# New priorities for both layers of a two-layer attention trunk, a mask that closes its score group, and work moved between ScalarE and VectorE

## The chip, the core and the metric

The kernel runs on one core of a Trainium2 chip. The metric is the time of one execution on the device, in microseconds (us). The engines of the core work at the same time, each through its own queue, in order: TensorE (PE, matrix products; its weight loads are listed as PEld), VectorE (DVE), ScalarE (ACT), GpSimd (POOL), and SyncE (SP), whose queue issues all loads and stores here. "span" is the time from the first to the last instruction of the profiled execution.

## The reference

256 positions of width 1024 go through two layers and a last RMSNorm, all in float32. Both layers have this form:

```python
hn = rmsnorm(h, norm_g[i])
q, k, v, z = split_proj(hn, w_in)            # one projection; 16 heads of 64
q, k = apply_rope(q, cos, sin), apply_rope(k, cos, sin)
o = attention(q, k, v)
o = o.reshape(B, S, MIX_WIDTH) * jax.nn.silu(z)
h = h + o @ w_out[i]
```

The first layer attends within a window of 128 positions, with 2 key and value heads and a learned sink for each query head that enters the softmax's sum. The second has 4 key and value heads and blocks of 256 keys. With 256 positions there is only one block, so it is causal attention over all of them.

## The kernel before

**Data.** Activations stand transposed: 8 tiles of 128 features by 256 positions. Weights come in 54 pieces of 512 KB, each 128 x 1024 (8 tiles of 128 x 128), in the order in which they are used: per layer query weights for the first half of the heads (q0), keys and values (kv), the second half (q1), the gate z in two halves (z0, z1), and the output projection in two halves (o0, o1); in the second layer kv comes before q0. All are loaded on SP's queue in this order (L84 to L90) into five raw buffers (`wraw`, NRAW = 5). A load waits until its buffer is free.

**Precision.** A float32 product is made from three matmuls in a faster format (`triple`, L136). The weight piece is split (`split`, L96): ScalarE copies its high part (`whi`, L108), and VectorE subtracts it to get the low part (`wlo`, L109). The activations are split in the same way (`split_h`, L147). Then come high x high, high x low and low x high (L140 to L142). For the pieces listed in `NATIVE`, nothing is split; TensorE multiplies float32 directly (L138), with unsplit activations `xf` (L155), and the piece keeps its raw buffer until TensorE is done with it. There are NHI = 7 buffers for high parts and NLO = 7 for low parts. With PACE = 2, the high part of a piece also waits until the low part of the piece two before it is written (L111).

Pieces are numbered in the order of `split` calls in the program: 0 to 3 are q0 of the first layer, 4 and 5 kv, 6 to 9 q1, 10 to 13 z0, 14 to 17 z1, 18 to 25 the output projection; 26 to 29 are kv of the second layer, 30 to 33 q0, 34 to 37 q1, 38 to 41 z0, 42 to 45 z1, and the rest the output projection.

**Statistics.** The squares of the input are summed, TensorE adds them over the partitions (L175), VectorE and GpSimd make the reciprocal root (L177, L179), and TensorE spreads it over all partitions (L182). It is multiplied into the rotation tables `csr` (L280), with which queries and keys are rotated (`rope`, L216): a shuffle and a multiplication on VectorE, and a second multiplication and an addition on VectorE or, for the entries in `RPL`, on GpSimd (L227, L228).

**Attention.** It goes in units of 4 heads by 128 queries: for each half c of the heads, u picks 4 of its 8 heads and b the first or the second 128 queries, so 8 units a layer. A unit with b = 1 sees 256 keys, one with b = 0 sees 128. In `attn` (L314), TensorE first adds the mask to the one score buffer (`sc`, L328), by a product of an identity with the mask in bf16, two matmuls over all of the unit's keys; then it adds the scores (L332). VectorE takes the maximum (L334), and ScalarE the exponentials with their sums (L343). VectorE makes the reciprocal (L346) and scales the four heads' probabilities (L348). TensorE transposes them (L353), ScalarE copies the transpose out of PSUM (L355), and TensorE multiplies by the values (L357). VectorE multiplies by the gate (L363), and the result is split for the output projection (L365, L366). There is one PSUM buffer for scores, one for the output `o`, two for transposes and three for projections (`mm`).

**Order.** Every instruction carries a priority, set by `at(...)` around each step from the tables `PRI0` and `PRI1` (plus 100 in the second layer). A planner orders the instructions before the kernel runs: it simulates the engines with durations of its own, and on each engine takes, of the instructions that are then ready and have their buffers, the one with the lowest number. On the chip, each engine follows that order strictly. The names in the tables are: `sq0`, `skv`, `sz0`, `so0` and so on for the splits of weights, `q0`, `kv`, `z0`, `o0` for the matmuls, `a0` and `a1` for the attention of each half, `st` for the statistics, `r0`, `r1`, `rk` for the rotations, `e0`, `e1` for what follows the gate's matmuls, and `f0`, `f1` for what follows the output projection's. `ORDER` and `ORDER1` give the order of the four units (b, u) in each half.

Of the kernel before, what the change touches and what calls it, by code (L numbers as in the profile page):

```python
# [17 lines left out]
T = S // P  # L18
TCX = {'schedule_with_timeline_sim': True}
SYNC = mybir.DependencyInfo(mybir.DependencyClass.Sync, mybir.DependencyReason.DATA)  # L20
PACE = 2
NATIVE = (7, 9, 11, 13, 15, 17, 31, 33, 35, 37, 39, 41)
RPL = [(0, 1, 0), (0, 1, 1), (1, 'k'), (1, 1, 0), (1, 1, 1)]
GLP = [(0, 0), (1, 0), (1, 1)]
SZP = [(0, 0), (0, 3), (1, 1)]
NRAW, NHI, NLO = 5, 7, 7
PRI0 = {'tr': -185.1, 'skv': -345.0, 'st': -372.0, 'kv': -93.4, 'sq0': -378.2, 'q0': -54.6, 'sz0': -416.4, 'z0': -41.1, 'a0': -142.2, 'sq1': -73.6, 'q1': -125.3, 'a1': -156.4, 'sz1': -158.0, 'z1': -31.1, 'so0': -360.9, 'o0': 17.2, 'so1': -103.2, 'o1': -39.6, 'r0': -138.0, 'r1': 21.5, 'rk': -107.9, 'p0': -118.5, 'p1': 29.8, 'e0': -99.9, 'e1': -247.7, 'f0': -197.9, 'f1': -254.0}
PRI1 = {'r0': -102.1, 'r1': -128.1, 'tr': 25.5, 'skv': -2.9, 'st': -281.7, 'kv': -97.4, 'sq0': -95.7, 'q0': -83.6, 'sz0': -20.3, 'z0': -7.5, 'a0': -176.2, 'sq1': -58.7, 'q1': -73.4, 'a1': -177.4, 'sz1': -74.6, 'z1': 87.9, 'so0': 80.5, 'o0': -32.3, 'so1': -88.6, 'o1': 91.0, 'rk': -31.6, 'p0': -215.2, 'p1': -14.3, 'e0': -145.1, 'e1': -189.1, 'f0': -90.9, 'f1': -119.3}
NPT = 3
NMM, NTR, NSC = 3, 2, 1  # L30
NW = 9
ORDER = [(0, 0), (1, 0), (1, 1), (0, 1)]
ORDER1 = [(0, 0), (0, 1), (1, 0), (1, 1)]
STEP = 0.1
EPS = 1e-05
NEG = -1e+30
# [3 lines left out]
def trunk(ctx: ExitStack, tc: tile.TileContext, xT, gf, sinks, consts, masks, wkva, w, out):  # L40
# [104 lines left out]
        return act.tile([P, 2, 2, S], F32R, name="quad", bufs=6)  # L145

    def split_h(layer, k, hs):  # L147
        if k == 0:
            xf.append(act.tile([P, KT, S], F32, name="xf", bufs=1))
        if k % 2 == 0:  # L150
            q = quads()
            hs += [q[:, 0], q[:, 1]]
        hi, lo = hs[k][:, 0], hs[k][:, 1]
        gc = g[:, layer, k:k + 1]
        nc.scalar.activation(xf[layer][:, k], h[:, k], AF.Copy, scale=gc)  # L155
        nc.scalar.activation(hi, h[:, k], AF.Copy, scale=gc)
        nc.vector.scalar_tensor_tensor(lo, h[:, k], gc, hi.bitcast(F32), op0=OP.mult, op1=OP.subtract)

# [33 lines left out]
    for layer in range(2):  # L192
# [18 lines left out]

        def block(ps, hw, j, k, width):
            wh, wl = cols(hw, j, k, width)
            triple(ps, wh, wl, hs[k][:, 0], hs[k][:, 1], xf[layer][:, k], k == 0, k == KT - 1)

        def rope(aps, pool=False, out=None):  # L216
            n = sum(x.shape[1] for x in aps)
# [96 lines left out]
        def attn(c, b, u, qs):  # L314
            nk = (b + 1) * P
            h0 = 8 * c + 4 * u
            if b == 0:
                mask = mkb[:, 2:3]
            else:
                mask = mkb[:, 1:3] if layer == 0 else mkb[:, 3:5]  # L320
            mask = mask.rearrange("p k s -> p (k s)")
            nm = work.tile([P, 4], F32, name="nm", bufs=4)
            rs = work.tile([P, 4], F32, name="rs", bufs=4)
            ri = work.tile([P, 4], F32, name="ri", bufs=4)
            p = work.tile([P, 4, nk], F32, name="pb" if b else "pa", bufs=2)
            sc = psum.tile([P, 2, 512], F32, name="sc", bufs=NSC)[:, :, :2 * nk].rearrange("p r (i k) -> p r i k", i=2)
            for par in range(2):
                nc.tensor.matmul(sc[:, par], mkb[:, 0], mask[:, None].to_broadcast([P, 2, nk]), start=True, stop=False)  # L328
            for n in range(4):
                i, par = n // 2, n % 2  # L330
                half = slice(64 * par, 64 * par + 64)
                nc.tensor.matmul(sc[:, par, i], qs[half, 2 * u + i, b * P:(b + 1) * P], ks[half, (h0 + n) // per, :nk],  # L332
                                 start=False, stop=i == 1)
            nc.vector.tensor_reduce(nm.rearrange("p (i r) -> p r i", r=2), sc, axis=mybir.AxisListType.X, op=OP.max,  # L334
                                    negate=True)
            scs = [sc[:, n % 2, n // 2] for n in range(4)]
            if layer == 0:
                es = work.tile([P, 4], F32, name="es", bufs=4)
                nc.vector.tensor_tensor(nm, nm, nsink[:, h0:h0 + 4], op=OP.min)
                nc.vector.tensor_add(es, nm, sink[:, h0:h0 + 4])  # L340
                nc.scalar.activation(es, es, AF.Exp)
            for n in range(4):
                nc.scalar.activation(p[:, n], scs[n], AF.Exp, bias=nm[:, n:n + 1], accum_out=rs[:, n:n + 1])  # L343
            if layer == 0:
                nc.vector.tensor_add(rs, rs, es)
            nc.vector.reciprocal(ri, rs)  # L346
            for n in range(4):
                nc.vector.tensor_scalar(p[:, n], p[:, n], ri[:, n:n + 1], None, op0=OP.mult)  # L348
            po = psum.tile([P, 2, P], F32, name="o", bufs=1)
            for kt in range(b + 1):  # L350
                pt = psum.tile([P, 4, P], F32, name="tr", bufs=NTR)
                for n in range(4):
                    nc.tensor.transpose(pt[:, n], p[:, n, kt * P:(kt + 1) * P], ident)  # L353
                pT = work.tile([P, 4, P], F32, name="pT", bufs=NPT)
                nc.scalar.activation(pT, pt, AF.Copy)  # L355
                for par in range(2):
                    nc.tensor.matmul(po[64 * par:64 * par + 64], vs[:, kt, h0 // per], pT[:, par::2],  # L357
                                     start=kt == 0, stop=kt == b)
            if (c, u) not in gt:
                gt[c, u] = quads()  # L360
            sl = slice(b * P, (b + 1) * P)
            gf = work.tile([P, 2, P], F32, name="gf")
            nc.vector.tensor_mul(gf, po, sz[:, 4 * c + 2 * u:4 * c + 2 * u + 2, sl])  # L363
            gh, gl = gt[c, u][:, :, 0, sl], gt[c, u][:, :, 1, sl]
            last[0] = nc.scalar.activation(gh, gf, AF.Copy)  # L365
            (nc.gpsimd if (c, u) in GLP else nc.vector).tensor_sub(gl, gf, gh.bitcast(F32))  # L366

        def zproj(c):
            with at(B + PRI["sz%d" % c]):
                hw = split(jz[c])  # L370
            with at(B + PRI["z%d" % c]):
                for f in range(4):
                    ps = psum.tile([P, S], F32, name="mm", bufs=NMM)
                    for k in range(KT):
                        c0 = f % 2 * P
                        wh, wl = part(hw[f // 2 * 2 + k // 4], k % 4, c0)
                        triple(ps, wh, wl, hs[k][:, 0], hs[k][:, 1], xf[layer][:, k], k == 0, k == KT - 1)
                    with at(B + PRI["e%d" % c]):
                        z = work.tile([P, S], F32, name="z")
                        th = work.tile([P, S], F32, name="th")  # L380
                        nc.vector.tensor_mul(z, ps, rh)
                        nc.scalar.activation(th, z, AF.Tanh)  # L382
                        if (c, f) in SZP:
                            nc.gpsimd.tensor_mul(th, th, z)  # L384
                            nc.gpsimd.tensor_add(sz[:, 4 * c + f], th, z)
                        else:
# [76 lines left out]
                                              o[:, 4 * i:4 * i + 4].rearrange("p k s -> p (k s)"))  # L463

        def attn_c(c, qs):
            for i, (b, u) in enumerate(ORDER if c == 0 else ORDER1):
                with at(B + PRI["a%d" % c] + STEP * i):
                    attn(c, b, u, qs)

# [83 lines left out]
```

## Time and profile before

| | |
|---|---|
| median of 3 runs | 244.24 us (241.94 to 244.81) |
| profiled execution, its own time | 243.5 us |
| its span | 241.7 us |
| mean granted TensorE clock | 0.984 |
| HBM read | 30.39 MB |

The rows of the profile read as follows. A group of instructions has its line, engine and operation, output<-input tiles, shapes and count, then the busy time, the mean of one in ns, and the idle time of the engine just before them with what ended it. A row of the timeline has the start, the duration, the engine, the line, and in brackets the idle time before it and its releaser. A row of the chain of waits has start, duration and instruction. A row of a windows table has, for each engine, busy time and instruction count, then the granted clock, the busy share of the DMA engines and GB/s. A row on waits has the total time, the number of times and the longest, in us.

### The profile page before, as it was taken

The numbers are of one execution on the slowest core, as the hardware profiler recorded it, in microseconds if no ns is written. First come the engines' busy times: TensorE is split into PE (matmuls) and PEld (weight loads), VectorE is DVE, ScalarE is ACT, GpSimd is POOL, SyncE is SP. The second block draws the span as 40 slices with busy tenths as digits, with TensorE's granted clock in tenths as the row PEclk, the third lists the DMA queues.
The fourth block names the chain that finished last, engine by engine and source line by source line (L and its number), as shares of the span: only waits on it lengthen the run. The fifth ranks groups of instructions, "written<-read, shape, count | busy, mean of one in ns | idle before, by whom it ended". The sixth has DMA issues, their size and how long they took to land.

```text
span 241.7 us, 4064 instructions
## 1 busy us (share of the span) xinstructions
PE 226.8 (94%) x1511; PEld 188.8 (78%) x1511; DVE 157.8 (65%) x321; ACT 125.2 (52%) x310; POOL 62.3 (26%) x64
## 2 busy tenths in 40 slices
PE   8979999999999999769999999999599999999990
PEld 4879989877678878559999988968487869687780
DVE  3899956938767867528972757585756556465363
ACT  7984245265765634529960624462656535474231
POOL 1872033232053011100741500030813103003241
PEclk9999999999999999999999999999799999999996
DMA  6998664444754222004743345247551420000022
GB/s 181 326 387 269 223 170 148 168 153 139 251 161 125 74 102 88 0 1 134 241 150 89 91 153 168 69 157 240 169 175 41 136 87 0 3 0 0 3 86 87
DMA packets 10244, 31.71 MB, mean 131 GB/s; under 512 B 1264, under 2 KB 2160, under 8 KB 10224
## 3 DMA queue, kind: packets, MB, share of 16 engines
q1 hardware_dynamic: 10224, 31.45, 40.5%
q8 instruction: 12, 0.20, 0.3%
q14 instruction: 8, 0.07, 0.1%
HBM read 30.39 MB, written 1.05 MB: 130 GB/s over the span
## 4 chain that ended last, share of the span: by engine, by line
PE 62%; DMA 15%; ACT 9%; DVE 8%; issue 2%; SPq 2%; POOL 1%; POOLq 0%; ACTq 0%; DVEq 0%
DMA wraw<-w 15%; PE mm L138 8%; PE mm L142 6%; PE mm L141 6%; PE mm L140 6%; PE tr L353 5%; PE sc L332 5%; PE o L357 5%; DVE wlo L109 4%; ACT whi L108 4%; PE mm L400 3%; PE mm L401 3%; PE mm L399 3%; PE mm L436 2%; PE mm L438 2%
## 5 line engine op out<-in xcount | busy, mean ns | idle before, releaser
L108 ACT ACTIVATE whi<-wraw 128x1024 fp32r<-128x1024 f32 (+2 forms) x45 | 44.7, 999 | 49.8 <-DMA wraw<-w 33.4
L109 DVE TENSOR_TENSOR wlo<-wraw,whi 128x1024 fp32r<-128x1024 f32 (+2 forms) x45 | 53.7, 1197 | 23.4 <-ACT whi L108 23.2
L140 PE MATMUL mm<-quad,whi 128*128 128x256 f32 x176 | 55.0, 315 | 0.8 <-ACT whi L108 0.8
L141 PE MATMUL mm<-quad,whi 128*128 128x256 f32 x176 | 50.1, 289 | 0.0
L142 PE MATMUL mm<-quad,wlo 128*128 128x256 f32 x176 | 49.2, 286 | 0.8 <-DVE wlo L109 0.8
L138 PE MATMUL mm<-xf,wraw 128*128 128x256 f32 x192 | 48.8, 388 | 0.0
L138 PEld LDWEIGHTS mm<-xf,wraw 128*128 128x128 f32 x192 | 34.3, 192 | 5.1 <-issue 1.4
L140 PEld LDWEIGHTS mm<-quad,whi 128*128 128x128 f32 x176 | 33.8, 193 | 3.3 <-ACT whi L108 1.3
L141 PEld LDWEIGHTS mm<-quad,whi 128*128 128x128 f32 x176 | 33.5, 192 | 2.5 <-issue 1.9
L142 PEld LDWEIGHTS mm<-quad,wlo 128*128 128x128 f32 x176 | 33.0, 190 | 1.9 <-DVE wlo L109 1.5
L366 POOL TENSOR_TENSOR quad<-gf,quad 128x256 fp32r<-128x256 f32 x12 | 10.5, 873 | 61.6 <-ACT quad L365 61.6
L355 ACT ACTIVATE pT<-tr 128x512 f32<-128x512 f32 x24 | 13.7, 594 | 21.7 <-PE tr L353 20.0
L334 DVE TENSOR_REDUCE nm<-sc 128x4 f32<-128x512 f32 (+1 forms) x16 | 15.2, 953 | 10.0 <-PE sc L332 10.0
L227 POOL TENSOR_TENSOR t<-t,csr 128x512 f32<-128x512 f32 x5 | 6.4, 1280 | 50.6 <-DVE t L223 46.9
L399 PE MATMUL mm<-quad,whi 128*128 128x256 f32 x64 | 17.7, 290 | 1.0 <-ACT quad L365 1.0
L332 PE MATMUL sc<-ks,qs 64*128 64x256 f32 (+1 forms) x128 | 18.6, 355 | 0.0
L400 PE MATMUL mm<-quad,whi 128*128 128x256 f32 x64 | 18.3, 290 | 0.2 <-POOL quad L366 0.2
L401 PE MATMUL mm<-quad,wlo 128*128 128x256 f32 x64 | 18.1, 287 | 0.0
L166 POOL TENSOR_TENSOR sq<-sq 128x256 f32<-128x256 f32 x14 | 14.7, 1052 | 8.4 <-ACT sq L164 7.8
L343 ACT ACTIVATE pb<-sc,nm 128x256 f32<-128x256 f32 x32 | 14.8, 472 | 3.7 <-DVE nm L334 3.7
L332 PEld LDWEIGHTS sc<-ks,qs 64*128 64x128 f32 x128 | 10.9, 186 | 6.7 <-issue 6.1
L384 POOL TENSOR_TENSOR th<-th,z 128x256 f32<-128x256 f32 x6 | 7.2, 1203 | 33.7 <-ACT th L382 33.7
(107 smaller groups left out, 412.1 us busy)
## 6 DMA issues: line engine op xcount, KB each, us to landing
wraw<-w SPq DMA_DIRECT2D x50, 512.0 KB, 4.5
wraw<-wkva SPq DMA_DIRECT2D x2, 512.0 KB, 8.6
out<-of SPq DMA_DIRECT2D x4, 256.0 KB, 2.2
wraw<-w SPq DMA_DIRECT2D x3, 256.0 KB, 3.8
hg<-xT SPq DMA_DIRECT2D x2, 256.0 KB, 5.7
wraw<-gf SPq DMA_DIRECT2D x1, 512.0 KB, 3.5
hg<-xT SPq DMA_DIRECT2D x3, 128.0 KB, 3.5
cst<-consts SPq DMA_DIRECT2D x1, 320.0 KB, 9.1
```

Of the source, the lines that this page charges most:

```text
L108: ia = nc.scalar.activation(a[:, c0:c1], r[:, c0:c1], AF.Copy)
L109: ib = nc.vector.tensor_sub(b[:, c0:c1], r[:, c0:c1], a[:, c0:c1].bitcast(F32))
L138: nc.tensor.matmul(ps, wh, x, start=start, stop=stop)
L140: nc.tensor.matmul(ps, wh, xh, start=start, stop=False)
L141: nc.tensor.matmul(ps, wh, xl, start=False, stop=False)
L142: nc.tensor.matmul(ps, wl, xh, start=False, stop=stop)
L332: nc.tensor.matmul(sc[:, par, i], qs[half, 2 * u + i, b * P:(b + 1) * P], ks[half, (h0 + n) // per, :nk], start=False, stop=i == 1)
L334: nc.vector.tensor_reduce(nm.rearrange("p (i r) -> p r i", r=2), sc, axis=mybir.AxisListType.X, op=OP.max, negate=True)
L343: nc.scalar.activation(p[:, n], scs[n], AF.Exp, bias=nm[:, n:n + 1], accum_out=rs[:, n:n + 1])
L399: nc.tensor.matmul(ps, wh, gh, start=k == 0, stop=False)
L400: nc.tensor.matmul(ps, wh, gl, start=False, stop=False)
L401: nc.tensor.matmul(ps, wl, gh, start=False, stop=k == 3)
```

## The change

- The priorities in `PRI0` and `PRI1` are all new, and the order of units is now given for each layer and half (`ORDERS`).
- PACE goes from 2 to 1, NHI from 7 to 9, and NLO from 7 to 5.
- `NATIVE` lists 10 pieces in place of 12, others in part.
- In `attn` the scores come first and the mask closes the group. In the second layer the mask covers only the last 128 keys, the diagonal block.
- For the units in `PSC`, ScalarE scales the probabilities in place of VectorE. For those in `PEV`, VectorE copies the transposes in place of ScalarE.
- `RPL`, `GLP` and `SZP`, which send work to GpSimd, have new entries, now by layer and unit: 3 rotations in place of 5, 10 subtractions in place of 12, and 6 gates as before.
- `xf` is written only in a layer that has a native piece among its projections; both layers have some.

```diff
-PACE = 2
-NATIVE = (7, 9, 11, 13, 15, 17, 31, 33, 35, 37, 39, 41)
-RPL = [(0, 1, 0), (0, 1, 1), (1, 'k'), (1, 1, 0), (1, 1, 1)]
-GLP = [(0, 0), (1, 0), (1, 1)]
-SZP = [(0, 0), (0, 3), (1, 1)]
-NRAW, NHI, NLO = 5, 7, 7
-PRI0 = {'tr': -185.1, 'skv': -345.0, 'st': -372.0, 'kv': -93.4, 'sq0': -378.2, 'q0': -54.6, 'sz0': -416.4, 'z0': -41.1, 'a0': -142.2, 'sq1': -73.6, 'q1': -125.3, 'a1': -156.4, 'sz1': -158.0, 'z1': -31.1, 'so0': -360.9, 'o0': 17.2, 'so1': -103.2, 'o1': -39.6, 'r0': -138.0, 'r1': 21.5, 'rk': -107.9, 'p0': -118.5, 'p1': 29.8, 'e0': -99.9, 'e1': -247.7, 'f0': -197.9, 'f1': -254.0}
-PRI1 = {'r0': -102.1, 'r1': -128.1, 'tr': 25.5, 'skv': -2.9, 'st': -281.7, 'kv': -97.4, 'sq0': -95.7, 'q0': -83.6, 'sz0': -20.3, 'z0': -7.5, 'a0': -176.2, 'sq1': -58.7, 'q1': -73.4, 'a1': -177.4, 'sz1': -74.6, 'z1': 87.9, 'so0': 80.5, 'o0': -32.3, 'so1': -88.6, 'o1': 91.0, 'rk': -31.6, 'p0': -215.2, 'p1': -14.3, 'e0': -145.1, 'e1': -189.1, 'f0': -90.9, 'f1': -119.3}
+PACE = 1
+NATIVE = (2, 5, 9, 13, 17, 28, 31, 33, 35, 39)
+RPL = [(0, 'k'), (1, 'k'), (1, 1, 1)]
+GLP = [(0, 0, 0, 0), (0, 0, 1, 0), (0, 0, 1, 1), (0, 1, 0, 1), (0, 1, 1, 0), (0, 1, 1, 1), (1, 0, 0, 1), (1, 0, 1, 1), (1, 1, 1, 0), (1, 1, 1, 1)]
+SZP = [(0, 0, 0), (0, 1, 1), (0, 1, 2), (1, 0, 0), (1, 1, 0), (1, 1, 1)]
+PSC = [(0, 0, 0, 0), (0, 1, 1, 0), (0, 1, 1, 1), (1, 0, 1, 1), (1, 1, 0, 0), (1, 1, 0, 1)]
+PEV = [(0, 0, 0, 1), (0, 0, 1, 0), (0, 0, 1, 1), (0, 1, 0, 0), (0, 1, 1, 0), (1, 0, 0, 1), (1, 0, 1, 0), (1, 1, 0, 1)]
+NRAW, NHI, NLO = 5, 9, 5
+PRI0 = {'tr': -287.9, 'skv': -62.3, 'st': 0.1, 'kv': -127.1, 'sq0': -336.8, 'q0': -207.0, 'sz0': -275.2, 'z0': 123.6, 'a0': -277.7, 'sq1': 30.6, 'q1': -208.2, 'a1': -67.4, 'sz1': 34.5, 'z1': -81.2, 'so0': -74.2, 'o0': 69.2, 'so1': -174.5, 'o1': -235.1, 'r0': -426.2, 'r1': -132.5, 'rk': -126.5, 'p0': -32.5, 'p1': 31.4, 'e0': -150.4, 'e1': 5.8, 'f0': -320.3, 'f1': 32.1}
+PRI1 = {'r0': -343.3, 'r1': 169.0, 'tr': -20.1, 'skv': -51.5, 'st': -246.0, 'kv': -155.5, 'sq0': -365.0, 'q0': -165.9, 'sz0': -41.4, 'z0': 35.1, 'a0': -262.3, 'sq1': -286.7, 'q1': -54.2, 'a1': -15.8, 'sz1': -3.4, 'z1': 133.0, 'so0': -252.4, 'o0': -80.4, 'so1': -53.1, 'o1': -121.2, 'rk': 209.6, 'p0': 73.0, 'p1': -293.4, 'e0': -131.5, 'e1': -274.8, 'f0': -419.3, 'f1': -225.4}
...
-ORDER = [(0, 0), (1, 0), (1, 1), (0, 1)]
-ORDER1 = [(0, 0), (0, 1), (1, 0), (1, 1)]
+ORDERS = [[[(1, 1), (1, 0), (0, 0), (0, 1)], [(1, 0), (0, 1), (0, 0), (1, 1)]], [[(0, 0), (1, 0), (1, 1), (0, 1)], [(1, 0), (0, 0), (0, 1), (1, 1)]]]
...
-            for par in range(2):
-                nc.tensor.matmul(sc[:, par], mkb[:, 0], mask[:, None].to_broadcast([P, 2, nk]), start=True, stop=False)
             for n in range(4):
                 i, par = n // 2, n % 2
                 half = slice(64 * par, 64 * par + 64)
                 nc.tensor.matmul(sc[:, par, i], qs[half, 2 * u + i, b * P:(b + 1) * P], ks[half, (h0 + n) // per, :nk],
-                                 start=False, stop=i == 1)
+                                 start=i == 0, stop=False)
+            k0 = nk - P if layer else 0
+            for par in range(2):
+                nc.tensor.matmul(sc[:, par, :, k0:], mkb[:, 0], mask[:, None, k0:].to_broadcast([P, 2, nk - k0]),
+                                 start=False, stop=True)
...
-                nc.vector.tensor_scalar(p[:, n], p[:, n], ri[:, n:n + 1], None, op0=OP.mult)
+                if (layer, c, b, u) in PSC:
+                    nc.scalar.activation(p[:, n], p[:, n], AF.Copy, scale=ri[:, n:n + 1])
+                else:
+                    nc.vector.tensor_scalar(p[:, n], p[:, n], ri[:, n:n + 1], None, op0=OP.mult)
...
-                nc.scalar.activation(pT, pt, AF.Copy)
+                if (layer, c, b, u) in PEV:
+                    nc.vector.tensor_copy(pT, pt)
+                else:
+                    nc.scalar.activation(pT, pt, AF.Copy)
```

More of the change, by code (lines that the diff above doesn't have):

```diff
@@ L147, in split_h @@
     def split_h(layer, k, hs):
+        whole = any(26 * layer <= j < 26 * layer + 20 for j in NATIVE)
         if k == 0:
-            xf.append(act.tile([P, KT, S], F32, name="xf", bufs=1))
+            xf.append(act.tile([P, KT, S], F32, name="xf", bufs=1) if whole else None)
         if k % 2 == 0:
@@ L154, in split_h @@
         gc = g[:, layer, k:k + 1]
-        nc.scalar.activation(xf[layer][:, k], h[:, k], AF.Copy, scale=gc)
+        if whole:
+            nc.scalar.activation(xf[layer][:, k], h[:, k], AF.Copy, scale=gc)
         nc.scalar.activation(hi, h[:, k], AF.Copy, scale=gc)
@@ L213, in block @@
             wh, wl = cols(hw, j, k, width)
-            triple(ps, wh, wl, hs[k][:, 0], hs[k][:, 1], xf[layer][:, k], k == 0, k == KT - 1)
+            triple(ps, wh, wl, hs[k][:, 0], hs[k][:, 1], None if wl is not None else xf[layer][:, k], k == 0, k == KT - 1)
         def rope(aps, pool=False, out=None):
@@ L365, in attn @@
             last[0] = nc.scalar.activation(gh, gf, AF.Copy)
-            (nc.gpsimd if (c, u) in GLP else nc.vector).tensor_sub(gl, gf, gh.bitcast(F32))
+            (nc.gpsimd if (layer, c, u, b) in GLP else nc.vector).tensor_sub(gl, gf, gh.bitcast(F32))
         def zproj(c):
@@ L376, in zproj @@
                         wh, wl = part(hw[f // 2 * 2 + k // 4], k % 4, c0)
-                        triple(ps, wh, wl, hs[k][:, 0], hs[k][:, 1], xf[layer][:, k], k == 0, k == KT - 1)
+                        triple(ps, wh, wl, hs[k][:, 0], hs[k][:, 1], None if wl is not None else xf[layer][:, k], k == 0, k == KT - 1)
                     with at(B + PRI["e%d" % c]):
@@ L382, in zproj @@
                         nc.scalar.activation(th, z, AF.Tanh)
-                        if (c, f) in SZP:
+                        if (layer, c, f) in SZP:
                             nc.gpsimd.tensor_mul(th, th, z)
@@ L465, in attn_c @@
         def attn_c(c, qs):
-            for i, (b, u) in enumerate(ORDER if c == 0 else ORDER1):
+            for i, (b, u) in enumerate(ORDERS[layer][c]):
                 with at(B + PRI["a%d" % c] + STEP * i):
```

## The prediction

> **What bounds the kernel now.** I read the page's engine table first, then the order of time on TensorE, then the stretches in which TensorE did not stream, and in each of these the engine that released it.
>
> ```profile
> span 241.7 us, 4064 instructions
> ...
> PE 226.8 (94%) x1511; PEld 188.8 (78%) x1511; DVE 157.8 (65%) x321; ACT 125.2 (52%) x310; POOL 62.3 (26%) x64
> ```
>
> TensorE is busy for 94% of the span, and the other three engines are far from full. But the durations of matmuls overlap, so 226.8 us isn't what TensorE needs. The distance from one start to the next is. The timeline of TensorE gives it for split weights, the chain of waits for native float32 weights:
>
> ```profile
> 57.40 0.28 PE L140 MATMUL mm<-quad,whi 128*128 128x256 f32 x1
> ...
> 57.76 0.28 PE L140 MATMUL mm<-quad,whi 128*128 128x256 f32 x1
> ```
> ```profile
> 58.28 1.73 PE mm L138 x8
> ```
>
> Three matmuls of a split weight tile (L140, L141, L142) take 57.76 - 57.40 = 0.36 us, 0.12 us each, where the rows say 0.28 us for one. Eight native ones take 1.73 us, 0.216 us each. TensorE streams like this almost throughout. What is left to win is fewer matmuls, and the holes. The largest three, as the timeline of TensorE shows them in brackets (idle time, and who ended it):
>
> ```profile
> 12.96 0.39 PE L140 MATMUL mm<-quad,whi 128*128 128x256 f32 x1 [0.84 <-ACT whi L108]
> ...
> 14.44 0.50 PE L142 MATMUL mm<-quad,wlo 128*128 128x256 f32 x2 [0.50 <-DVE wlo L109]
> ...
> 101.58 0.38 PE L328 MATMUL sc<-mkb 128*128 128x256 bf16 x2 [1.08 <-ACT pb L343]
> ...
> 102.93 0.63 PE L353 MATMUL tr<-cst,pb 128*128 128x128 f32 x4 [0.43 <-DVE pb L348]
> ...
> 106.43 1.14 PE L357 MATMUL o<-pT,vs 128*64 128x256 f32 x8 [0.64 <-ACT pT L355]
> ...
> 108.61 0.62 PE L399 MATMUL mm<-quad,whi 128*128 128x256 f32 x3 [1.04 <-ACT quad L365]
> ...
> 168.19 1.03 PE L138 MATMUL mm<-xf,wraw 128*128 128x256 f32 x4
> 171.70 0.38 PE L328 MATMUL sc<-mkb 128*128 128x256 bf16 x2 [2.48 <-ACT pb L343]
> ```
>
> First hole (front): TensorE waits for the split of a weight piece. Second (99 to 109 us, the end of the first layer): the last attention units have no projection left to run beside them, and the chain softmax, transpose, copy, product, gate stands open, 1.08 + 0.43 + 0.64 + 1.04 = 3.2 us in these rows. Third (second layer): 2.48 us, the longest. Its cause is on ScalarE and VectorE:
>
> ```profile
> 162.66 1.22 DVE L334 TENSOR_REDUCE nm<-sc 128x4 f32<-128x1024 f32 x1
> ```
> ```profile
> 165.62 1.06 ACT L108 ACTIVATE whi<-wraw 128x1024 fp32r<-128x1024 f32 x1 [3.08 <-DMA wraw<-w]
> 168.76 1.06 ACT L108 ACTIVATE whi<-wraw 128x1024 fp32r<-128x1024 f32 x1 [2.08 <-DMA wraw<-w]
> 169.73 0.46 ACT L343 ACTIVATE pb<-sc,nm 128x256 f32<-128x256 f32 x1
> ```
>
> The maxima were there at 162.66 + 1.22 = 163.88 us, but the exponentials start at 169.73: on ScalarE two weight splits stood ahead of them, and waited 3.08 and 2.08 us for their loads. The only score buffer stayed taken, so the next scores on TensorE stood still. The windows behind the hole (last-but-two column: granted clock) show a second cost:
>
> ```profile
> 172.00:174.00 2.00, 2.00 (x12) 1.61 (x12) 2.00 (x6) 1.36 (x2) 1.43 (x3) 0.69 0.77 227
> 174.00:176.00 2.00, 2.00 (x11) 1.79 (x9) 1.75 (x3) 0.54 (x3) 1.41 (x1) 0.50 0.17 53
> 176.00:178.00 2.00, 2.00 (x16) 1.97 (x15) 0.96 (x5) 1.76 (x8) 0.00 (x0) 0.95 0.79 213
> ```
>
> The clock fell to 0.50: 2 x (0.31 + 0.50 + 0.05) = 1.7 us of matmul time lost. This hole cost 2.48 + 1.7 = 4.2 us.
>
> **The change part by part.** The profiled execution took 243.5 us (span 241.7), 0.74 us under the median of 244.24. I sum against 243.5 and add 0.74 at the end.
>
> Work on TensorE. A piece of weights holds 8 tiles, so 24 split matmuls (24 x 0.12 = 2.88 us) or 16 native instructions (16 x 0.216 = 3.46 us). Ten native pieces in place of twelve: 2 x 0.58 = -1.2 us. The mask, by the chain of waits (512 columns, then 256):
>
> ```profile
> 95.46 0.45 PE sc L328 x2
> ...
> 180.19 0.24 PE sc L328 x2
> ```
>
> In the second layer the four units with b = 1 now mask 256 columns a matmul and not 512: 4 x (0.45 - 0.24) = -0.8 us. That the mask closes the group costs nothing: the same instructions stand between the free score buffer and the maximum, and the first of them, now a score, waits for that buffer as the mask did. Where TensorE streams both terms count in full: -2.0 us. Ends: 0 (if all of it falls into waits) and -2.0; I take the full one, since the timeline shows few waits.
>
> Front. Piece 2, the third of the first query weights, becomes native, and so needs no split:
>
> ```profile
> 11.85 1.06 ACT L108 ACTIVATE whi<-wraw 128x1024 fp32r<-128x1024 f32 x1
> ```
> ```profile
> 12.94 1.45 DVE L109 TENSOR_TENSOR wlo<-wraw,whi 128x1024 fp32r<-128x1024 f32 x1
> ```
>
> These two are what the 0.84 and 0.50 us at 12.96 and 14.44 us waited for. Its native matmuls need xf, which ScalarE writes ahead of them as before (both layers keep native pieces, so the new guard on xf takes nothing out). They cover 3.46 us, in which the next piece's split (1.06 + 1.45) fits. So -1.3 us; ends 0 (the hole moves to piece 3) and -1.3.
>
> VectorE, ScalarE, GpSimd. By groups:
>
> ```profile
> L109 DVE TENSOR_TENSOR wlo<-wraw,whi 128x1024 fp32r<-128x1024 f32 x40 | 50.1, 1253 | 22.7 <-ACT whi L108 22.5
> L348 DVE TENSOR_SCALAR pb<-pb,ri 128x256 f32<-128x256 f32 x32 | 12.0, 435 | 0.2
> ...
> L348 DVE TENSOR_SCALAR pa<-pa,ri 128x128 f32<-128x128 f32 x32 | 8.2, 315 | 0.2
> ...
> L224 DVE TENSOR_TENSOR qs<-mm,csr 128x512 f32<-128x512 f32 x6 | 4.0, 674 | 0.0
> ```
> ```profile
> L108 ACT ACTIVATE whi<-wraw 128x1024 fp32r<-128x1024 f32 x40 | 42.1, 1057 | 49.5 <-DMA wraw<-w 33.1 <-PE mm L276 8.3 <-DVE wlo L109 4.6
> ...
> L355 ACT ACTIVATE pT<-tr 128x512 f32<-128x512 f32 x24 | 13.7, 594 | 21.7 <-PE tr L353 20.0 <-PE o L357 1.7
> L155 ACT ACTIVATE xf<-hg 128x256 f32<-128x256 f32 x16 | 8.0, 498 | 0.8 <-DMA hg<-xT 0.7
> ```
> ```profile
> L227 POOL TENSOR_TENSOR t<-t,csr 128x512 f32<-128x512 f32 x5 | 6.4, 1280 | 50.6 <-DVE t L223 46.9 <-DVE csr L280 3.7
> ```
>
> Six units' scalings leave VectorE, 12 x 0.435 + 12 x 0.315 = 9.0 us, and cost ScalarE at most 24 x 0.498 = 12 us (its scaled copy of 256 columns; half of these have 128). Twelve copies of transposed probabilities go the other way: 12 x 0.594 = 7.1 us off ScalarE, about 12 x 0.674 = 8.1 us on VectorE (its nearest row that reads 512 columns of PSUM). Two more split pieces add 2 x 1.06 and 2 x 1.25 us. Three query rotations, two operations each, come back from GpSimd (1.28 us a multiplication there; here about the 0.674 us of L224, so 6 x 0.674 = 4.0 us). The first layer's key rotation goes there, and two more small subtractions come to VectorE, under 1 us each way. VectorE ends near 163 us, ScalarE near 132 us at most: still with room. What hides this is TensorE's stream. Without cover the scalings of one unit on ScalarE cost 4 x (0.498 - 0.435) = 0.25 us; the last unit of the first layer (among the six) stands open, so +0.25 us, ends 0 and 1.
>
> Priorities, unit order, pace, buffers. The loads keep their order on SP; their times follow from when buffers come free. PACE 1 makes each split on ScalarE wait for the low part of the piece just before it (none if that is native): the exponentials queued behind it wait too, and their score buffer with them. Pieces 37 and 41 of the second layer are no longer native, so they hold a raw buffer only until they are split, and the loads that came late at 165 to 169 us can start sooner. The waits of the load queue bear on it:
>
> ```profile
> SPq L84 <- DVE wlo L109: 56.5, 20, 8.5
> ...
> SPq L84 <- PE mm L138: 20.7, 7, 9.6
> ```
>
> Loads stood 20.7 us for native matmuls to free a raw buffer. So I take the third hole as mostly gone: of 4.2 us, 3.5 (a new order leaves some wait; the ends are -4.2 and +7.6, below). The Trainium skill, "TensorE: Matmul & The Clock Gate", section on what is actually happening, says that the clock falls back after at least one idle window of about 3.4 us; this trace shows half clock after 2.48 us, so the measurement decides. By the page the dip would not be this hole's, and the sum would keep 1.7 us more: 239.4 us in place of 237.7.
>
> The second hole I leave at 0. There z1 now stands ahead of the second half's attention, which takes cover from its end, while z0 falls behind everything and gives cover back; ends -3.2 and +3.2 (gone, or doubled).
>
> Sum: 243.5 - 2.0 - 1.3 - 3.5 + 0.25 = 236.95; with 0.74, **237.7 us**.
>
> **Rivals.** *The holes only move.* The third hole is one late load ahead of exponentials in a strict order; another order may meet another late load. Then the fewer matmuls and the front remain: 243.5 - 3.3 + 0.74 = 240.9 us. For it: loads wait for buffers all through (56.5 us). Against: the other holes quoted are made of waits of at most 1.08 us.
>
> *Stock of split weights (slower).* NLO falls from 7 to 5, so low parts can stand two pieces less ahead of TensorE, and raw buffers are freed later. Where TensorE drains the stock, as at 168 us, it waits for two pieces more: 2 x 2.88 = 5.8 us, and behind it the clock loses 1.7 to 1.8 us again. 243.5 - 3.3 + 0.25 + 7.6 + 0.74 = 248.8 us, with the old hole still there. For it: the 20 waits on wlo. Against: NHI rises, fewer native pieces hold raw buffers, and the hole comes from one slot. It decides when the low buffers are all taken while a load stands ready.
>
> *Late statistics in the first layer.* Their priority goes from -372 to 0.1, behind q0, kv and q1. The three matmul buffers stay taken by q0 and kv until the rotations have read them, and these need the statistics:
>
> ```profile
> 16.80 0.61 PE L175 MATMUL tr<-one,sq 128*128 128x2 f32 x4
> ```
> ```profile
> 18.89 0.14 DVE L177 TENSOR_SCALAR ms<-tr 128x2 f32<-128x2 f32 x1
> ...
> 23.48 0.74 DVE L224 TENSOR_TENSOR qs<-mm,csr 128x256 f32<-128x256 f32 x2
> ```
>
> The chain from 16.80 to 24.22 us, 7.4 us, lies under matmuls now. Started only when these are done, it stands open, without the 18.89 - 17.41 = 1.5 us for which it queued behind splits on VectorE: 237.7 + 5.9 = 243.6 us. Against: TensorE waits for splits in the front anyway, and work of low priority runs in a hole.
>
> **How the numbers follow.** Two per cent of 244.24 is 4.9 us, about what a measurement of this kernel can tell from no change: below 239.4 is faster, above 249.1 slower. Forecast 0.46 (own range 233 to 241), moved holes 0.26, late statistics 0.10, stock 0.18 (spread over 245 to 253, since less or more than two pieces may lack). Faster: 0.40 of the forecast's chance and 0.04 of the moved holes', 0.44. Slower: half of the stock's, 0.09, and 0.04 where the stock and the late statistics fall together (248.8 + 5.9), 0.13. The rest, 0.43, is within. The range begins at 232, a little under the case in which both later holes go (243.5 - 2.0 - 1.3 - 4.2 - 3.2 + 0.25 + 0.74 = 233.8). It ends at 248, which leaves out the dearer half of the stock's case and the two together, 0.13 to 0.15.
>
> **What would show it.** Native matmuls have 160 rows in place of 192 (8 of them in the second layer's value projection); the mask has 24 of 256 columns and 8 of 512. At 11 to 15 us no wait on whi or wlo over 0.3 us. No TensorE hole over 1.5 us between 110 and 229 us, and a clock of 1.00 there. VectorE near 163, ScalarE near 132 us. Wrong would be a hole of over 2 us with a dip behind it in the second layer (holes move, or stock), or TensorE idle between L175 and L182 (late statistics).

## The result and the profile after

The changed kernel takes 228.16 us (median of 4 runs, 227.43 to 230.13), and the kernel before, run beside it, 244.53 us. The ratio is 0.938 (95% interval 0.9285 to 0.9476): 16.4 us less, over twice the forecast 6.5, and below the range. The profiled execution took 230.13 us, the longest of the four.

The head of the page of the changed kernel (busy time, share of the span, instructions):

```profile
span 228.3 us, 4102 instructions
...
PE 218.0 (95%) x1527; PEld 187.5 (82%) x1527; DVE 161.8 (71%) x317; ACT 129.1 (57%) x324; POOL 52.6 (23%) x58
```

VectorE and ScalarE are as busy as the sum had them (163 and at most 132 us). TensorE's busy time falls by 8.8 us. Its timeline at the places of the three holes (line numbers have moved by one or more: the statistics' first matmuls are L178, L410 and L411 are the output projection of the first layer):

```profile
9.88 0.51 PE L143 MATMUL mm<-quad,wlo 128*128 128x256 f32 x2 [0.52 <-DVE wlo L110]
17.25 0.61 PE L178 MATMUL tr<-one,sq 128*128 128x2 f32 x4 [1.39 <-POOL sq L169]
...
104.36 0.62 PE L410 MATMUL mm<-quad,whi 128*128 128x256 f32 x3 [1.04 <-ACT quad L376]
105.17 0.38 PE L411 MATMUL mm<-quad,whi 128*128 128x256 f32 x1 [0.19 <-POOL quad L377]
```

These are all the waits that the timeline names behind its first row, 3.1 us together, where before there were 7.9. In the second layer there is none. Its windows there (busy time of the five engines, granted clock, DMA share, GB/s):

```profile
168.00:174.00 6.00, 6.00 (x51) 4.97 (x48) 4.31 (x11) 3.45 (x12) 0.29 (x1) 1.00 0.40 142
174.00:180.00 6.00, 6.00 (x51) 4.83 (x51) 4.26 (x8) 3.18 (x9) 0.62 (x1) 1.00 0.30 90
```

TensorE is busy throughout, at full clock. Waits explain 4.8 us of the 13.4 between the spans of the two profiled executions. The rest shows when each group of TensorE's timeline is counted from its start to the next start, less the idle time named (the row of transposes takes in all of TensorE's):

| TensorE, us | before | after |
|---|---|---|
| named idle time | 7.9 | 3.1 |
| scores and transposes | 31.4 | 25.6 |
| mask | 6.7 | 3.6 |
| all else | 195.7 | 196.0 |

Both columns hold one stretch at half clock, which costs 1.7 us: behind the third hole before, and behind the wait of 1.39 us in the profiled execution of the changed kernel (last section).

Scores and transposes take 5.8 us less, though their number is the same. About 0.7 of that is the low clock before (eight transposes at 174 us took 1.57 us, at 200 us in the changed kernel 0.85). The remainder goes with their order. A unit of the second layer before, mask, scores and another unit's transposes in turn:

```profile
158.62 0.59 PE L328 MATMUL sc<-mkb 128*128 128x512 bf16 x2
159.14 0.70 PE L332 MATMUL sc<-ks,qs 64*128 64x256 f32 x2
159.77 0.66 PE L353 MATMUL tr<-cst,pb 128*128 128x128 f32 x4
160.36 0.70 PE L332 MATMUL sc<-ks,qs 64*128 64x256 f32 x2
160.98 0.66 PE L353 MATMUL tr<-cst,pb 128*128 128x128 f32 x4
161.57 0.70 PE L332 MATMUL sc<-ks,qs 64*128 64x256 f32 x4
162.20 0.48 PE L138 MATMUL mm<-xf,wraw 128*128 128x256 f32 x1
```

and the same work in the changed kernel, in two places:

```profile
189.90 1.13 PE L333 MATMUL sc<-ks,qs 64*128 64x256 f32 x8
190.96 0.39 PE L337 MATMUL sc<-mkb 128*128 128x256 bf16 x2
191.11 0.36 PE L142 MATMUL mm<-quad,whi 128*128 128x256 f32 x1
...
200.04 1.09 PE L361 MATMUL tr<-cst,pb 128*128 128x128 f32 x8
200.89 0.36 PE L143 MATMUL mm<-quad,wlo 128*128 128x256 f32 x1
```

Scores and transposes stand 162.20 - 159.14 = 3.06 us before, and 1.06 + 0.85 = 1.91 us after, without any wait in brackets. In TensorE's instruction list before, a score follows a transpose, or the reverse, 18 times, in the changed kernel once.

### The profile page after: what moved, and what is told of

Same layout as the page of the kernel before. It is cut to its first block, busy times and chain, and to the rows that moved or that the text cites. A ratio compares the mean times of both kernels' runs of the same rounds, so it can differ in the third digit from the quotient of the medians.

```text
span 228.3 us, 4102 instructions
## 1 busy us (share of the span) xinstructions
PE 218.0 (95%) x1527; PEld 187.5 (82%) x1527; DVE 161.8 (71%) x317; ACT 129.1 (57%) x324; POOL 52.6 (23%) x58
## 4 chain that ended last, share of the span: by engine, by line
PE 80%; POOL 5%; DVE 5%; issue 4%; DMA 3%; ACT 1%; POOLq 0%; ACTq 0%; DVEq 0%
PE mm L139 11%; PE mm L142 10%; PE mm L141 9%; PE mm L143 9%; PE o L368 6%; PE sc L333 6%; PE tr L361 5%; PE mm L410 4%; PE mm L411 3%; PE mm L412 3%; POOL sq L169 3%; PE mm L447 2%; PE mm L449 2%; PE mm L448 2%; PE sc L337 2%
## 5 line engine op out<-in xcount | busy, mean ns | idle before, releaser
L141 PE MATMUL mm<-quad,whi 128*128 128x256 f32 x200 | 60.4, 305 | 0.1
L143 PE MATMUL mm<-quad,wlo 128*128 128x256 f32 x200 | 57.5, 292 | 0.5 <-DVE wlo L110 0.5
L142 PE MATMUL mm<-quad,whi 128*128 128x256 f32 x200 | 57.4, 290 | 0.0
L142 PEld LDWEIGHTS mm<-quad,whi 128*128 128x128 f32 x200 | 38.3, 192 | 1.7 <-issue 1.1
L141 PEld LDWEIGHTS mm<-quad,whi 128*128 128x128 f32 x200 | 38.5, 193 | 1.3 <-ACT whi L109 0.5
L143 PEld LDWEIGHTS mm<-quad,wlo 128*128 128x128 f32 x200 | 38.1, 193 | 0.9 <-DVE wlo L110 0.7
L139 PE MATMUL mm<-xf,wraw 128*128 128x256 f32 x144 | 35.4, 380 | 0.0
L139 PEld LDWEIGHTS mm<-xf,wraw 128*128 128x128 f32 x144 | 25.6, 190 | 3.0 <-issue 0.4
L339 DVE TENSOR_REDUCE nm<-sc 128x4 f32<-128x1024 f32 (+1 forms) x16 | 15.3, 955 | 7.9 <-PE sc L337 7.8
L410 PE MATMUL mm<-quad,whi 128*128 128x256 f32 x64 | 17.7, 295 | 1.0 <-ACT quad L376 1.0
L411 PE MATMUL mm<-quad,whi 128*128 128x256 f32 x64 | 18.1, 288 | 0.2 <-POOL quad L377 0.2
L412 PE MATMUL mm<-quad,wlo 128*128 128x256 f32 x64 | 17.8, 284 | 0.0
L333 PE MATMUL sc<-ks,qs 64*128 64x256 f32 (+1 forms) x128 | 16.0, 354 | 0.0
L160 DVE SCALAR_TENSOR_TENSOR quad<-hg,quad 128x256 fp32r<-128x256 f32 x16 | 11.7, 739 | 4.4 <-ACT quad L159 4.3
L368 PE MATMUL o<-pT,vs 128*64 128x256 f32 x96 | 14.3, 398 | 0.0
L410 PEld LDWEIGHTS mm<-quad,whi 128*128 128x128 f32 x64 | 11.7, 191 | 3.2 <-ACT quad L376 1.5
L333 PEld LDWEIGHTS sc<-ks,qs 64*128 64x128 f32 x128 | 10.1, 186 | 4.9 <-issue 2.5
```

Of the source, the lines that this page charges most:

```text
L139: nc.tensor.matmul(ps, wh, x, start=start, stop=stop)
L141: nc.tensor.matmul(ps, wh, xh, start=start, stop=False)
L142: nc.tensor.matmul(ps, wh, xl, start=False, stop=False)
L143: nc.tensor.matmul(ps, wl, xh, start=False, stop=stop)
L410: nc.tensor.matmul(ps, wh, gh, start=k == 0, stop=False)
L411: nc.tensor.matmul(ps, wh, gl, start=False, stop=False)
```

## The experiments

Kernels of different sessions are compared by their ratio to the kernel before, which ran beside each. The intervals of the ratios are about 0.01 to either side, and 0.01 is 2.4 us.

**Which part carries the gain.** The first four undo or do one part.

e1, the mask first again and over all keys:

```diff
+            for par in range(2):
+                nc.tensor.matmul(sc[:, par], mkb[:, 0], mask[:, None].to_broadcast([P, 2, nk]), start=True, stop=False)
             for n in range(4):
...
-            k0 = nk - P if layer else 0
-            for par in range(2): ...
```

> The changed kernel with the mask first again and over all keys in both layers. By the work alone (the prediction's term) it is 0.8 us slower than the changed kernel, about 229.0. If the place of the mask matters by itself (in the timelines a mask pair ahead of the scores takes 0.53 us of TensorE for 512 columns and 0.32 for 256, behind the scores 0.25 and 0.15, with about 0.1 us more at the joins), it is 2.5 to 3 us slower, about 231, and the mask's starts lie 0.26 us apart again. Above 233 the new plan was made for the new place of the mask, and the loss is the plan's.

231.09 us, ratio 0.945: slower by 1.7 us by the ratios and 2.9 by the medians, not separable from the changed kernel by the intervals. In its trace the mask's rows take 6.4 us from start to start, not 3.6, and 0.8 of that is the width by the prediction's rows. So the place costs something, as the second theory has it, but its size has to come from the strip below.

e2, the old priorities and unit orders:

```diff
-PRI0 = {'tr': -287.9, 'skv': -62.3, 'st': 0.1, ...}
+PRI0 = {'tr': -185.1, 'skv': -345.0, 'st': -372.0, ...}
...
-ORDERS = [[[(1, 1), (1, 0), (0, 0), (0, 1)], ...
+ORDERS = [[[(0, 0), (1, 0), (1, 1), (0, 1)], [(0, 0), (0, 1), (1, 0), (1, 1)]]] * 2
```

> The changed kernel with the priorities and unit orders of before; pieces, pace, buffers, mask and moved work stay new. If the priorities carry the gain, 236 to 242, with holes of over 1 us on TensorE again. If the settings that decide when loads and splits come carry it, at most 231, without the long hole in the second layer.

236.42 us, ratio 0.969: half of the gain is left. The second layer has no long hole.

e3, the new priorities and unit orders on the kernel before:

```diff
-PRI0 = {'tr': -185.1, 'skv': -345.0, 'st': -372.0, ...}
+PRI0 = {'tr': -287.9, 'skv': -62.3, 'st': 0.1, ...}
...
-ORDER = ...
+ORDERS = ...
```

> The kernel before with the new priorities and unit orders alone. If the priorities carry the gain, at most 236. If they are worth something only with the rest, 240 to 248, with splits on ScalarE that wait for loads ahead of exponentials.

Ratio 1.02 (1.007 to 1.032): not faster, rather slower. The new order by itself is worth nothing on the old settings.

e4, the old settings in the changed kernel:

```diff
-PACE = 1
-NATIVE = (2, 5, 9, 13, 17, 28, 31, 33, 35, 39)
-NRAW, NHI, NLO = 5, 9, 5
+PACE = 2
+NATIVE = (7, 9, 11, 13, 15, 17, 31, 33, 35, 37, 39, 41)
+NRAW, NHI, NLO = 5, 7, 7
```

> The changed kernel with the native pieces, the pace and the split buffers of before. By work alone 1.2 us slower, 229.4. If pace and pieces took away the waits for loads on ScalarE, the long hole is back: 233 or more, and the idle time of ScalarE's splits is ended by loads and not by VectorE.

247.35 us, ratio 1.014: the whole gain is gone. The long hole is back, with its cause. TensorE's timeline of e4, then ScalarE's, then the windows behind the hole:

```profile
174.78 0.72 PE L333 MATMUL sc<-ks,qs 64*128 64x128 f32 x8 [3.77 <-ACT pb L348]
```
```profile
167.73 1.06 ACT L109 ACTIVATE whi<-wraw 128x1024 fp32r<-128x1024 f32 x1 [3.94 <-DMA wraw<-w]
171.85 1.06 ACT L109 ACTIVATE whi<-wraw 128x1024 fp32r<-128x1024 f32 x1 [3.07 <-DMA wraw<-w]
```
```profile
176.00:178.00 2.00, 2.00 (x10) 1.69 (x9) 0.58 (x2) 2.00 (x5) 0.85 (x2) 0.53 0.64 215
178.00:180.00 2.00, 2.00 (x13) 2.00 (x13) 2.00 (x3) 1.80 (x9) 0.60 (x1) 0.62 0.65 217
```

Splits on ScalarE wait for loads ahead of the exponentials, TensorE stands 3.77 us, and the clock falls, as the prediction read it in the kernel before. What ends the splits' idle time, before and in the changed kernel:

```profile
ACT whi L108 <- DMA wraw<-w: 33.4, 17, 5.2
...
ACT whi L108 <- DVE wlo L109: 4.6, 3, 3.1
```
```profile
ACT whi L109 <- DVE wlo L110: 30.6, 19, 4.9
ACT whi L109 <- DMA wraw<-w: 16.8, 6, 9.0
```

Splits wait half as long for loads now, and for VectorE instead.

**Which setting.** e5 to e7 undo one of the three in the changed kernel, and e8 puts the three into the kernel before.

```diff
-PACE = 1
+PACE = 2
```

> The changed kernel with PACE 2 alone (e4 undid pace, pieces and buffers together and lost 19 us). If the pace keeps splits from standing on ScalarE ahead of exponentials while their load is on its way, most of the 19 us is lost: 238 or more, and ScalarE's splits wait for loads (33 us in e4, 17 in the changed kernel). If the pieces or buffers matter, at most 232.

```diff
-NATIVE = (2, 5, 9, 13, 17, 28, 31, 33, 35, 39)
+NATIVE = (7, 9, 11, 13, 15, 17, 31, 33, 35, 37, 39, 41)
```

> The changed kernel with the twelve native pieces of before alone. By the work 1.2 us slower, 229.4. If native pieces that keep raw buffers make the loads late, 236 or more, with load waits on native matmuls at 20 us or above (10 to 20 us in the changed kernel).

```diff
-NRAW, NHI, NLO = 5, 9, 5
+NRAW, NHI, NLO = 5, 7, 7
```

> The changed kernel with 7 and 7 split buffers in place of 9 and 5, alone. By the slower rival of the prediction (the stock of low parts), two more low buffers can only help: 224 to 228. If the buffers carry part of the gain, 232 or more. If they don't matter, 227 to 230.

240.73, 239.91 and 240.55 us (0.980, 0.977, 0.982): each undone setting loses about 10 us. But none of the three has the long hole in the second layer. Two of the settings are enough against it. Their loss is made of smaller waits (7.5 to 9.3 us of named idle time) and of scores and transposes (28.1 to 30.2 us). For e5 the split's waits for loads rise only to 23.8 us, from 16.8. For e6 loads wait 16.4 us for native matmuls, less than in the changed kernel (10.1 + 6.1 + 3.5 = 19.7 us over its three groups). So the mechanism expected of e5 is there in part and that of e6 is not, and the size has another source.

```diff
-PACE = 2
-NATIVE = (7, 9, 11, 13, 15, 17, 31, 33, 35, 37, 39, 41)
-NRAW, NHI, NLO = 5, 7, 7
+PACE = 1
+NATIVE = (2, 5, 9, 13, 17, 28, 31, 33, 35, 39)
+NRAW, NHI, NLO = 5, 9, 5
```

> The kernel before with the new pieces, pace and buffers alone: old priorities, mask and division of work. If these settings carry the gain by themselves, 230 to 234. If they need the new order and the moved work, 238 or more.

235.1 us, ratio 0.959 (0.953 to 0.965): the three settings alone, with the old priorities, mask and division of work, bring some 10 us. Named idle time falls to 4.9 us; scores and transposes stay at 28.4.

**How much hangs on the plan.** Every edit makes the planner order everything anew. Three runs ask what another plan costs.

e10, the old division of work in the changed kernel:

```diff
-PSC = [(0, 0, 0, 0), ...
-PEV = [(0, 0, 0, 1), ...
+PSC = []
+PEV = []
```

with GpSimd's three lists as before.

> The changed kernel with the old division of work: no scalings on ScalarE, no copies on VectorE, GpSimd's entries as before. By the prediction's terms, which hide all of this, 227 to 230. If the moved work shortens the waits within a unit, or keeps transposes together, 233 or more.

240.44 us, ratio 0.986, 11.7 us slower than the changed kernel by the ratios. The prediction had put this work at a loss of 0.25 us.

e11, e8 with the new priorities and unit orders added:

```diff
-PRI0 = {'tr': -185.1, ...
+PRI0 = {'tr': -287.9, ...
```

> The kernel before with the new pieces, pace and buffers and the new priorities and unit orders; old mask and old division of work. Settings alone gave 235.1 (e8). If the order adds its 8 us (e2) on its own, 227 to 231, mask included. If it does so only with the moved work and the mask, 234 or more.

237.54 us, ratio 0.979 (0.971 to 0.986): without moved work and mask, the new order brings nothing beyond e8 and loses some 5 us.

e12, the control, with both tables shaken:

```diff
-PRI0 = {'tr': -287.9, 'skv': -62.3, ...}
+PRI0 = {each number moved at random by up to 100}
```

> Control: the changed kernel with each priority moved at random by up to 100, all else new. If any other plan of these settings loses what e5 to e7 lost (12 us), those three show the loss of the plan and not of the setting: 238 to 242. If the settings hold most of the gain under another order, 230 to 236, as with the old priorities (e2, 236.4).

236.91 us, ratio 0.975: with all other edits kept, more than a third of the gain holds under this one random order, and 9 us are lost. So of the 10 us that e5 to e7 lost, and the 12 of e10, up to 9 can be the plan's, and what pace, pieces, buffers and moved work each cost by themselves stays open. The 19 us of e4 are twice that.

**What a worse plan costs on TensorE.** e9 sets a strip of matmuls behind the changed kernel's last product; it leaves nothing out:

```diff
+    for i in range(2):
+        for names in ("SSSSTTTT", "STTSTTSS", "MMSSSS", "SSSSMM", "SSSSHH"):
+            seq(names, pps, pss, ptr)      # S score, T transpose, M mask of 512, H mask of 256
+            seq("p" * 6, pps, pss, ptr)    # six split matmuls
```

> The changed kernel, and behind its last product a strip of matmuls on copies of late data (no output changes): four float32 scores of 64 x 256 and four transposes in a block (SSSSTTTT) or alternating (S TT S TT SS), a mask pair of 512 columns ahead of or behind the scores, a mask pair of 256 columns behind, each between split matmuls. If alternating forms cost TensorE time by themselves, the alternating strip takes over 1 us more than the block; if not, within 0.1 us. If a mask behind the scores is cheaper by its place, MMSSSS takes 0.2 us more than SSSSMM; narrowing gives SSSSHH 0.2 us less than SSSSMM.

TensorE's timeline (a score is two rows; L524 scores, L529 transposes, L534 masks, L518 split matmuls):

```profile
226.10 1.13 PE L524 MATMUL sc<-prb 64*128 64x256 f32 x8
227.17 0.66 PE L529 MATMUL tr<-cst,prb 128*128 128x128 f32 x4
227.58 0.96 PE L518 MATMUL mm<-prr 128*128 128x256 f32 x6
228.47 0.70 PE L524 MATMUL sc<-prb 64*128 64x256 f32 x2
229.09 0.44 PE L529 MATMUL tr<-cst,prb 128*128 128x128 f32 x2
229.46 0.70 PE L524 MATMUL sc<-prb 64*128 64x256 f32 x2
230.09 0.44 PE L529 MATMUL tr<-cst,prb 128*128 128x128 f32 x2
230.46 0.70 PE L524 MATMUL sc<-prb 64*128 64x256 f32 x4
231.09 0.98 PE L518 MATMUL mm<-prr 128*128 128x256 f32 x6
231.91 0.61 PE L534 MATMUL sc<-mkb 128*128 128x512 bf16 x2
...
234.41 1.14 PE L524 MATMUL sc<-prb 64*128 64x256 f32 x8
...
236.73 1.13 PE L524 MATMUL sc<-prb 64*128 64x256 f32 x8
...
238.83 1.13 PE L524 MATMUL sc<-prb 64*128 64x256 f32 x8
```

From strip to strip: the block takes 228.47 - 226.10 = 2.37 us, the alternating strip 231.91 - 228.47 = 3.44. That is 1.07 us more for the same work, with no wait on anybody, and the second pass of the strips repeats both within 0.01 us. It is not one price per change of form. Four scores in a row take 227.17 - 226.10 = 1.07 us. Apart, a lone score takes 0.62 or 0.63 us, and so do the two adjacent ones at 230.46: 0.62 + 0.63 + 0.63 = 1.88. Adjacent scores use different halves of the partitions (`half`), and in the trace their rows start in pairs, within 0.01 us of each other; the two rows of a lone score start 0.32 us apart. So 0.81 us are scores that lost their partner, and 0.33 us are transposes in pairs between scores (0.37 + 0.37) and not in a row of four (0.41); the split matmuls behind give back 0.07. The rows of the second layer above show the same: 0.63 and 0.62 us for lone scores, 0.63 for two, 1.06 for four. Whether two adjacent scores on one half would pair wasn't tried. The mask ahead of the scores takes 2.50 us, behind them 2.32; 0.09 of the difference is the join to the strip before, where a mask starts sooner behind a split matmul than a score does. So its place is worth about 0.1 us a unit, by estimate 1.6 us over 16. Narrowing gives 2.32 - 2.10 = 0.22 us a unit, as the sum had it.

**Alternation in whole kernels.** The same edit in four kernels puts a unit's scores and mask ahead of all other work, to keep transposes from falling between them:

```diff
-            for n in range(4):
-                ... scores and mask
+            with at(B - 2000):
+                for n in range(4):
+                    ... scores and mask
```

> e12 (shaken order, 236.9) with one thing more: the scores and the mask of a unit get a priority ahead of all else, so that they stand in a block. In the planned order of TensorE, changes from score to transpose or back fall from 12 to 0. If alternation costs by itself (1.1 us for four changes in the strip of e9), TensorE's time for scores and transposes falls from 29.2 to about 25.5 us and the median to 233 to 234. If the loss of the shaken order is all in waits, 236 to 238 again.

e13 (on e12): 229.12 us, ratio 0.938 after 0.975. Scores and transposes fall from 29.2 to 25.1 us, named idle time from 7.2 to 4.5, and a stretch at half clock of 3.4 us (at 106 us in e12) is gone.

> e10 (old division of work, 240.4) with scores and mask ahead of all else; changes fall from 11 to 1. By alternation, scores and transposes fall from 30.2 to about 26 us, and the median to 236 to 237. What is then left above the changed kernel is waits that the old division makes.

e16 (on e10): 233.3 us, ratio 0.956 after 0.986. Scores and transposes fall from 30.2 to 25.0 us, named idle time from 8.7 to 6.3.

> The kernel before with mask and scores ahead of all else; changes in the order fall from 18 to 10 (its old settings stay, and with them the long hole in the second layer, if these make it). By the alternation alone 2 us faster, about 242; no change if the wait for the reduced probabilities is what holds the transposes.

e15 (on the kernel before): 241.23 us, ratio 0.987 (0.979 to 0.995). Scores and transposes fall from 31.4 to 27.8 us. The waits stay, and so does the long hole of the old settings, 1.98 us here. In its profiled execution the clock falls to half three times for 3.4 us, once before.

> The changed kernel with scores and mask ahead of all else. It has one such change in its order, so the block wins nothing by itself: 227 to 229 if the plan stays as good, 230 to 234 if scores that come at once push projections back and open waits.

e14 (on the changed kernel): 229.22 us, ratio 0.939. Where almost nothing alternates, the edit brings nothing.

So alternation is a cost of its own. e13 also shows that one line of priorities does, for this random order, what the tuned tables do. e13 and e16 gained more than the alternation, since waits fell too; whether waits fall because TensorE gets through sooner wasn't tried.

**The front.** e17 and e18 tie the first layer's statistics on TensorE behind the first products of the keys, e17 with scores in a block, e18 without:

```diff
+        with (tc.issue_after(anchor.ins) if anchor is not None else ExitStack()):
             for t in range(T):
                 for i in range(len(a)):
                     nc.tensor.matmul(ps[:, t], a[i][:, t * P:(t + 1) * P], one, ...)
```

> e14 (scores and mask ahead of all else, 229.2) with the first layer's statistics tied behind the first products of the keys on TensorE, so that TensorE does not wait for GpSimd's squares at 15 us (1.35 us in e14). If that hole is pure loss and the new plan keeps scores and transposes apart, 227 to 228. If the statistics then come too late for the rotations, 230 or more, with TensorE idle before the second half's query products.

> The changed kernel with the same tie and no other edit. The wait of 1.39 us at 15 us goes: 226.5 to 227.5 if the plan stays as good. If the new plan is worse elsewhere, as in e12, 232 to 237.

234.57 and 235.12 us (0.962 and 0.964): slower than the changed kernel by some 6 us. The planner set the statistics behind all of the keys' products. TensorE's timeline of e17 shows two waits on their chain, and the windows the clock behind it:

```profile
27.19 0.71 PE L187 MATMUL tr<-cst,rstd 128*128 128x128 f32 x4 [1.09 <-POOL rstd L184]
30.20 0.55 PE L142 MATMUL mm<-quad,whi 128*128 128x256 f32 x1 [2.30 <-DVE qs L229]
```
```profile
30.00:33.00 3.00, 2.80 (x13) 2.83 (x14) 3.00 (x8) 0.37 (x1) 0.00 (x0) 0.50 0.88 310
33.00:36.00 3.00, 3.00 (x16) 3.00 (x16) 2.01 (x6) 1.74 (x2) 1.14 (x2) 0.50 0.57 193
```

After L187 comes the second wait, 2.30 us for a rotation on VectorE, and then half clock for 6 us, 3 us lost: 1.09 + 2.30 + 3 = 6.4 us. Neither run answers what it was made for, whether the changed kernel's wait of 1.39 us can be had back. They do show what the rival of late statistics costs when it happens.

## Why the prediction was wrong, point by point

Its direction was right, and its size was not. The step that failed is this, on TensorE: "TensorE streams like this almost throughout. What is left to win is fewer matmuls, and the holes." I had measured the distance of starts for the projections and taken it for the attention's matmuls too. There, before, scores that stood alone between transposes stretched it without a bracket that names a wait. That term was missing from the sum; between the two profiled executions it measured 5.8 us, 5.1 without the clock.

- *Fewer and narrower matmuls, -2.0.* The counts are right: the changed kernel has 144 + 8 + 8 = 160 native rows, and the narrower mask saves 0.22 us a unit in the strip, against 0.21 in the sum. The 1.2 us for native pieces were not measured alone. "All else", less the half clock in it (1.7 - 0.7 us before, 1.7 after), is 194.7 and 194.3 us, so 0.4 less is what shows.
- *The mask's place, 0.* Mis-sized: about 0.1 us a unit, by estimate a gain of 1.6 us. The sentence that "the same instructions stand between" counted instructions and not the joins between forms.
- *Front, -1.3.* Wrong. The waits that it named are gone, but TensorE stands 1.39 us for the statistics and 0.52 for a split, so named idle time there is not less, 1.9 us against 1.7. In the profiled execution 1.7 us of half clock come behind it. So the hole moved, as the end of 0 had it, not to piece 3 but to the squares on GpSimd, for which the statistics' matmuls wait. The new priority of the statistics isn't the cause: e2 and e8 have the old one and wait 1.22 and 1.30 us at the same place. The wait goes with the new list of native pieces: all kernels with the old list wait 0.8 to 1.7 us for a split at 13 us and none for the squares, and all with the new list and free statistics wait 0.2 to 1.8 us for the squares. What sets its size stays open.
- *VectorE, ScalarE, GpSimd, +0.25.* The busy times came out. But the moved work was not free to leave out: e10 loses some 12 us without it. More than half of that comes back with scores in a block (e16), so the loss came through TensorE's order more than through the load of the engines. How much of it is the work's own is open, since a random order loses 9 us (e12). "What hides this is TensorE's stream" left out that an edit here also changes that stream's order.
- *Third hole, -3.5.* Right in mechanism, and small in size: all 4.2 us went. e4 brings hole, cause and low clock back, and e8 takes it away with the settings alone. The reason given, native pieces that free raw buffers sooner, isn't shown to be the one, and the waits over the whole span don't bear it out: loads wait 19.7 us for native matmuls in the changed kernel, 20.7 before. Any two of the three settings do it (e5, e6, e7), with the rest of the change kept.
- *Second hole, 0.* 3.2 us before, 3.4 with a row of 0.19 us at 109.42; 1.04 + 0.19 = 1.2 us after: 2.2 us gained. It was put at 0 as two shifts that might cancel, without a row that weighs them. What closed it wasn't tried alone: with the old order (e2) 4.7 us stand there, with the settings alone (e8) 2.2.
- *Scores and transposes, no term.* 5.8 us gained, of which 0.7 is the clock behind the third hole.

The rivals: "the holes only move" holds for e3 and e4, and in the change for the front alone. The stock of split weights didn't show on TensorE, which waits 0.52 us for low parts in the whole span, though loads wait 84.1 us for low parts to be written in place of 56.5; e7 gives back the low buffers but also takes two high ones, and so doesn't test this alone. "Late statistics" didn't happen in the changed kernel: their first matmuls start at 17.25 us, 16.80 before. It was priced at 5.9 us of waiting, and e17 lost about that, against e14, but as 3.4 us of waits and 3 us of half clock, so that the number agrees by luck. The rule of the Trainium skill ("TensorE: Matmul & The Clock Gate", its part on what is actually happening), an idle window of about 3.4 us before the clock falls, would allow the dip of e4 behind 3.77 us, but not the one in e4 behind 2.13 us nor the kernel before's behind 2.48 us. The traces decide for shorter holes.

The range failed with the missing term: its low end, 232, took all holes as gone and stopped there.

## What to carry to other kernels

When TensorE looks full, compare the distance of starts with the bare one for each form of matmul, not for the largest group alone: a stretched distance with no wait beside it can be the order of the forms. Keep matmuls of one form together, above all those that use different halves of the partitions, with a priority if a planner orders them, before tuning anything finer. And when an edit goes through a planner, run a shaken plan as a control, or the loss of the plan is read as the worth of the edit.

## What the runs showed of the hardware that was not expected

- Two adjacent float32 scores on different halves of the partitions take TensorE 0.63 us, no longer than a lone one between transposes (0.62 us), and four take 1.07 (e9). Breaking the pairs costs time without any named wait. In the kernel before 20 of the 128 score rows start without a partner within 0.02 us, in the changed kernel 4.
- The granted clock fell to 0.50 behind holes of 2.48 us (before), 3.77 and 2.13 us (e4), and of 1.09 and 2.30 us close together (e17). Between the start of the kernel and TensorE's last product, each such stretch in these traces lasted 3.4 us, or twice that (e3, e17, e18). A hole of 1.39 us was followed by such a dip in the profiled execution of the changed kernel, and holes of 1.41 and 1.35 us in e13 and e14 were not. Windows of the changed kernel and of e14:

```profile
18.00:22.00 4.00, 4.00 (x24) 4.00 (x23) 2.24 (x8) 1.06 (x1) 1.71 (x1) 0.59 0.93 334
```
```profile
18.00:22.00 4.00, 4.00 (x36) 4.00 (x36) 3.10 (x11) 1.06 (x1) 1.70 (x1) 1.00 0.94 307
```

That is 4 x 0.41 = 1.6 us, most of the 2.0 us by which the profiled execution lies above the median of its kernel. The six executions on record fall in line: two with a mean clock of 0.99 took 230.1 and 230.4 us, four with 0.995 or more 227.1 to 228.2.
